# Modulation steps over both halves of each FFN, and a fifth direct block

## The chip, the core and the metric

The kernel runs on one core of a Trainium2 chip. PE is the matrix engine, with its weight loads shown apart; DVE, ACT and POOL are the vector, scalar and general-purpose engines; SP issues most of the DMAs. The time is device microseconds of one execution; a kernel's time is the median of its runs.

## What is computed

Two layers act on 256 latent and 256 context tokens of width 1024 (batch 1), with the same weights for both streams: a half-step SwiGLU feed-forward network (FFN) of 2816 hidden features, a mixer of three head groups, and a second FFN. Each branch has a norm whose shift and scale, and a gate, come from a modulation vector: nine rows of 1024 for each layer and stream, computed from the conditioning vectors.

```python
mod_x = (silu(c) @ ada_w[layer] + ada_b[layer]).reshape(b, 9, 1, d)
mod_c = (silu(c_ctx) @ ada_w[layer] + ada_b[layer]).reshape(1, 9, 1, d)
def ffn_branch(h, mod, i, nw, w1, w2):
    return h + 0.5 * mod[:, i + 2] * swiglu(ada_rms(h, nw, mod[:, i], mod[:, i + 1]), w1, w2)
x   = ffn_branch(x,   mod_x, 0, ...)      # then the mixer with rows 3, 4, 5, then
ctx = ffn_branch(ctx, mod_c, 0, ...)      # ffn_branch(..., 6, ...)
```

The second layer returns latent tokens alone, so its rows 5 to 8 are needed for one stream only.

## The kernel before

**Stages.** There are four FFNs, named here A (layer 0, first), B (layer 0, second), C (layer 1, first) and D (layer 1, second), with a mixer between A and B and between C and D. Tokens of both streams lie side by side, 512 columns; D has the latent 256 columns and two more for the shift.

**One FFN.** Its hidden features are done in two halves of eleven blocks of 128. A half has eleven blocks of the first matrix (a gate product and an up product, each of eight tiles deep) and then eight output tiles of the second matrix, eleven products each. A product is three matmuls, since every weight and activation is split into a high and a low part. The second half ends in a split tail: its last two output tiles are done for latent tokens first and then for context tokens, and the norm of the next stage begins in between.

**Strassen.** In B and C most first-matrix blocks are done by class `Seven`, a scheme with seven half-size products for eight (84 matmuls of 256 columns for 48 of 512). It needs sums of the activations, made once by `sums` on DVE and ACT in the lead of the FFN, and for each block weight sums made by accumulating DMAs of POOL and by DVE. `DIRECT` says how many blocks at the start of B's and C's first half are done directly while the sums are made.

**Weights.** `Stream` (L64) brings chunks in: SP loads a raw chunk (three buffers), ACT casts the high half `wh` (L89), DVE subtracts for the low half `wl` (L100), four buffers each, two chunks for an output tile. Second-matrix weights are prepared one tile ahead. The engines work in the order in which the instructions were written.

**Background steps.** The modulation of the later rows is done by DVE: a block of 128 output rows is a 128 x 1024 tile loaded by DMA, multiplied by the conditioning vector and summed, one instruction (a step, L290) for each stream, followed by a short read of the accumulator; after eight blocks of a row a finish of one or two short instructions. `ada_steps` (L264) lists the loads, steps and finishes; a step issues the load of a block as many blocks ahead as there are buffers. The list `bg` is worked off by `pump` (L185), which each product calls: it adds `pace` for every 512 columns and writes out an entry for each whole one; `drain_bg` writes out all that are left. Layer 0's 112 steps and the first 48 of layer 1 run in A at `APACE`, those of `ADA1` elsewhere: 28 in B's second half and 29 in C's second half with four buffers and loads by POOL, spread up to the tail's last tile, and seven in D's first half with loads by SP.

**Order around the change.** In a second half a tile's products are followed by the result add on DVE (`xT`, L441), the squares for the next norm on ACT (`sq`, L337) and their sum on DVE (`acc`, L341); the next tile's casts and low halves are written after them. In a first half there are no squares. From the sixth tile of B's and C's first half on, SP and POOL also load the weights of the first Strassen block of the second half (`seven.load`, `seven.add`), into the pair of buffers named `aw`.

Of the kernel before, what the change touches and what calls it, by code (L numbers as in the profile page):

```python
# [9 lines left out]
F32 = mybir.dt.float32  # L10
# [10 lines left out]
KT = D // 128  # L21
FF = 2816
JH = FF // 128 // 2
# [12 lines left out]
CHUNK = 1024  # L36
ADA_BUFS = 5

DIRECT = {(0, 1): (4, 0), (1, 0): (4, 0)}

ADA1 = {(0, 0): 48, (0, 1): 27, (1, 0): 29, (1, 1): 8}

STAT, OS, FS, SPR = 3, 3.5, 2, 12

# [6 lines left out]

NM = (4, 2)

SUMS = 1.0
GPACE = (0.4, 0.55)
OPACE = (0.8, 0.8)
APACE = 0.355
NPACE = (0.95, 1.0)
RPACE = (1.2, 1.4)

# [74 lines left out]
def tile_hybrid_dit(ctx: ExitStack, tc: tile.TileContext, t_x, t_c, t_cb, t_ada0, t_ada, t_adab, t_nw, t_w1, t_w2,  # L135
                    t_wi, t_wo, t_qkw, t_bias, t_sgw, t_sgb, t_lnwb, t_lg, t_gnw, t_tab, t_id, t_sel, out):
    nc = tc.nc
    V, S, G, PE, SP = nc.vector, nc.scalar, nc.gpsimd, nc.tensor, nc.sync
# [9 lines left out]
    def mm_bank(name="mm"):  # L148
        return bank("mm", 4, name)
# [8 lines left out]
    for l in range(L):  # L158
        for f in range(2):
            if f == 1:  # L160
                chunks += [t_wi[l, i] for i in WI[l]] + [t_wo[l, m] for m in range(KT)]
            for half in range(2):
                for j in range(DIRECT.get((l, f), (JH, JH))[half]):
                    chunks += [t_w1[l, f, half * JH + j, 0], t_w1[l, f, half * JH + j, 1]]
# [5 lines left out]
    bg = []  # L170
    pace = [0.0, 0.0]
# [26 lines left out]
    def drain_bg(n=None):  # L198
        while bg and (n is None or n > 0):
            bg.pop(0)()  # L200
            if n is not None:
                n -= 1
# [16 lines left out]
    with tc.manual_schedule():  # L219
# [39 lines left out]
        adap = [None, 0, SP, None]  # L259
# [4 lines left out]
        def ada_steps(l, count):  # L264

            def streams(r):

                return 1 if l == L - 1 and r > 4 else 2  # L270

            todo = []
            while ada_todo[l] and sum(streams(r) for r, b in todo) < count:
                todo.append(ada_todo[l].pop(0))
            tiles = {}
            nload = [0]

            def loads(n):
                while nload[0] < min(n, len(todo)):
                    r, b = todo[nload[0]]  # L280
                    t = tiles[r, b] = adap[0](nload[0])
                    adap[2].dma_start(out=t, in_=t_ada[l, r, b])
                    nload[0] += 1

            def step(i, s, n):
                loads(i + adap[1])
                r, b = todo[i]
                t = tiles[r, b]
                junk = adap[3].tile([128, CHUNK], F32, tag="cu", name="junk", bufs=1) if s < n - 1 else t
                V.tensor_tensor_reduce(out=junk, in0=t, in1=cb[:, s], scale=1.0, scalar=0.0, op0=ALU.mult, op1=ALU.add,  # L290
                                       accum_out=mod[l][:, 8 * r + b, s:s + 1])

            def fin(r, n):
                mo = mod[l][:, 8 * r:8 * r + 8, 0:n]
                V.tensor_tensor(out=mo, in0=mo, in1=adab[:, l, 8 * r:8 * r + 8].unsqueeze(2).to_broadcast([128, KT, n]),
                                op=ALU.add)
                i, k = divmod(r, 3)
                if k == 1:
                    V.scalar_tensor_tensor(out=amul[l][:, i, :, 0:n], in0=mo, scalar=1.0,
                                           in1=nw[:, l, i, :].unsqueeze(2).to_broadcast([128, KT, n]),  # L300
                                           op0=ALU.add, op1=ALU.mult)
                elif k == 2 and i != 1:
                    V.tensor_scalar(out=mo, in0=mo, scalar1=0.5, scalar2=None, op0=ALU.mult)

            out = [lambda: loads(adap[1])]
            for i, (r, b) in enumerate(todo):
                n = streams(r)
                out += [lambda i=i, s=s, n=n: step(i, s, n) for s in range(n)]
                if b == KT - 1:
                    out.append(lambda r=r, n=n: fin(r, n))  # L310
            return out
# [313 lines left out]
        def ffn(l, f, lead, norms, steps=None, tail=None):  # L625


            i = 2 * f
            one = lead == "one"
# [3 lines left out]
            with ExitStack() as es:  # L633
                fp = es.enter_context(tc.tile_pool(name="ffn", bufs=1))
                seven = None
                direct = DIRECT.get((l, f), (JH, JH))

# [4 lines left out]
                def seven_pool():  # L642
                    nonlocal seven
                    pool = es.enter_context(tc.tile_pool(name="seven", bufs=1))
                    seven = Seven(pool, fp, l, f)

                if (l, f) in DIRECT:
                    seven_pool()
                else:
                    nb = ADA_BUFS - one  # L650
                    adap[:] = lambda i: fp.tile([128, CHUNK], F32, tag="aw", name="aw", bufs=nb), nb, SP, fp
                if one:
                    bg.extend(ada_steps(1, ADA1[l, f]))
                    pace[0], pace[1] = len(bg) / (KT * (JH - 1)), 0.0
                for half in range(2):
                    aTh = fp.tile([128, JH, NT], F32R, tag="aTh", name="aTh")
# [33 lines left out]
                    if half == 0 and not one:  # L690
# [10 lines left out]
                        if seven:  # L701
                            bg.extend([s for q in range(2) for s in seven.sums(q)])
                            bg.append(lambda: seven.load_u(direct[0]))
                            pace[0], pace[1] = SUMS, 0.0
                        for j in range(2):
# [9 lines left out]
                    for j in range(j0, j1):  # L715
# [4 lines left out]
                        if lead_in and j == j1 - 1:  # L720
                            bg.extend(seven.prepare(n1))
                            pace[0], pace[1] = SUMS, 0.0
                        wg, wu = ws.take(), ws.take(AHEAD - 1)
# [46 lines left out]
                    def down(m, wa, wb, a, b, ps):  # L770
                        for kt in range(JH):
                            w, c = (wa, kt) if kt < 6 else (wb, kt - 6)
                            product(ps[:, a:b], w, 128 * c, aTh, aTl, (slice(None), kt, slice(a, b)),
                                    kt == 0, kt == JH - 1)

                    split_tail = half == 1 and len(streams) == 2
                    if one and half == 0:
                        drain_bg()
                    if seven and half:

                        aw = seven.pool.tile([128, 4, CHUNK], F32, tag="th", name="aw")
                        adap[:] = lambda i: aw[:, i % 4], 4, G, seven.pool
                        bg.extend(ada_steps(1, ADA1[l, f]))
                        pace[0], pace[1] = len(bg) / (JH * (KT - 1)), 0.0
                    ahead = seven and half == 0
                    for m in range(KT - 2 if split_tail else KT):
                        a, b = 0, T * len(streams)
                        wa, wb = ws.take(), ws.take(AHEAD - 1)
                        ps = mm_bank("d")
                        if ahead and m == KT - 3:  # L790
                            seven.load(JH)
                            seven.load(JH + 1)
                            seven.add(JH)
                            seven.add(JH + 1)
                        down(m, wa, wb, a, b, ps)
                        if ahead and m >= KT - 2:
                            for s in seven.prepare(JH)[slice(0, 4) if m == KT - 2 else slice(4, 7)]:
                                s()
                        residual(l, i, m, ps, 0, streams)
                        if half == 1:  # L800
                            for s in streams:
                                if s in norms:
                                    norms[s].add(m)
                            if tail:
                                tail(m)
# [768 lines left out]
        def start(fp, ps, up):  # L1574
# [91 lines left out]
            ws.auto = True  # L1666
            pace[0], pace[1] = APACE, 0.0
            return w
# [30 lines left out]
        for l in range(L):  # L1699
            last = l == L - 1  # L1700
            n1 = {s: Norm(l, 1, s) for s in range(2)}
            n2 = {s: Norm(l, 2, s) for s in range(1 if last else 2)}
            n3 = {} if last else {s: Norm(l + 1, 0, s) for s in range(2)}
            if l == 0:
                bg.extend(ada_steps(0, 112) + ada_steps(1, ADA1[0, 0]))
                bg.insert(1, small_inputs)
                bg.insert(2, lambda: S.activation(out=cb, in_=cb, func=AF.Silu))
                bg.insert(15, prepare)
                pace[0] = 0.0
            ffn(l, 0, "ffn" if l else "start", n1, FFN_TO_MIX)  # L1710
            mixer(l, n2)
            if l == 0:
                ffn(l, 1, "mix", n3, FFN_TO_FFN)
            else:
                def store(m):
                    SP.dma_start(out=out[:, m, :], in_=xT[:, m, 0:T])

                ffn(l, 1, "one", {}, tail=store)
# [117 lines left out]
```

## Time and profile before

| | us |
|---|---|
| runs before | 1841.72, 1845.37, 1847.55 |
| median of the runs | 1845.37 |
| profiled execution | 1841.88 |
| its span | 1840.1 |
| PE, DVE, ACT, POOL busy in the span | 1791.2, 1310.0, 729.4, 262.2 |
| mean granted clock of PE | 0.994 |

The span is the time from the first to the last instruction. All times in rows are microseconds from its start. In a line of instructions the bracket behind a row is the time for which the engine stood idle before it, and what ended that. A granted clock of 1.00 is 2.4 GHz and one of 0.50 is 1.2 GHz. Stretches named in the text: A's second-matrix products of the second half are at 341.8 to 412.1, B's at 1000.6 to 1071.1, C's at 1364.3 to 1439.4; those of B's first half at 828.5 to 890.1 and of C's at 1192.2 to 1253.8; D's first blocks at 1645 to 1710.

### The profile page before, as it was taken

What the parts mean: (1) busy time and instruction counts of PE and PEld (TensorE: products, weight loads), DVE (VectorE), ACT (ScalarE), POOL (GpSimd) and SP (SyncE); (2) the same over time, 40 slices, a digit from 0 to 9 for tenths busy, and PEclk for the clock granted to TensorE, in tenths of its full rate; (3) what the DMA queues carried; (4) which work ended last, traced back from release to release, by engine and by line L of the source; (5) the groups of instructions that cost most, each with busy time, mean ns of one, the idle gap of its engine ahead of it and who ended that gap; (6) DMA issues with size and microseconds to landing.
All of it is one profiled execution on the core that took longest, in us unless ns stands there. A gap on an engine that the chain in (4) does not pass through costs nothing. (4 is left out here: it accounts for less than half of the span.)

```text
span 1840.1 us, 29560 instructions
## 1 busy us (share of the span) xinstructions
PE 1791.2 (97%) x11592; PEld 1556.0 (85%) x11592; DVE 1310.0 (71%) x2214; ACT 729.4 (40%) x1211; POOL 262.2 (14%) x302
## 2 busy tenths in 40 slices
PE   7999999999999999999999999999998999999999
PEld 5787888888668989998999789989996867989999
DVE  5799988886454556783688977836888744667665
ACT  3422222225543234452354245424442555354443
POOL 0000000002014310220322102102212104310000
PEclk9999999999999999999999999999999999999999
DMA  8666766634211121753765626536659432346655
GB/s 310 237 196 221 259 211 215 195 130 149 78 55 47 49 78 58 189 130 124 178 177 175 199 83 169 143 114 184 170 184 317 148 104 76 95 144 234 197 172 157
DMA packets 104763, 292.19 MB, mean 159 GB/s; under 512 B 12208, under 2 KB 18992, under 8 KB 104496
## 3 DMA queue, kind: packets, MB, share of 16 engines
q1 hardware_dynamic: 88352, 249.93, 41.1%
q0 software_dynamic: 16272, 40.38, 10.1%
q8 instruction: 91, 1.49, 0.3%
q14 instruction: 48, 0.39, 0.1%
HBM read 289.21 MB, written 1.05 MB: 158 GB/s over the span
## 5 line engine op out<-in xcount | busy, mean ns | idle before, releaser
L100 DVE TENSOR_TENSOR wl<-wr,wh 128x1024 fp32r<-128x1024 f32 (+2 forms) x304 | 321.9, 1086 | 104.1 <-ACT wh L89 102.7
L89 ACT CAST wh<-wr 128x1024 fp32r<-128x1024 f32 (+2 forms) x304 | 275.8, 932 | 170.4 <-PE d L207 93.7
L206 PE MATMUL d<-aTh,wh 128*128 128x512 f32 (+1 forms) x770 | 273.5, 355 | 12.3 <-ACT wh L89 12.1
L208 PE MATMUL d<-aTh,wl 128*128 128x512 f32 (+1 forms) x770 | 272.8, 354 | 1.9 <-DVE wl L100 1.9
L207 PE MATMUL d<-aTl,wh 128*128 128x512 f32 (+1 forms) x770 | 271.9, 353 | 0.2 <-DVE aTl L682 0.2
L206 PEld LDWEIGHTS d<-aTh,wh 128*128 128x128 f32 x770 | 148.4, 193 | 35.3 <-ACT wh L89 14.1
L208 PEld LDWEIGHTS d<-aTh,wl 128*128 128x128 f32 x770 | 148.0, 192 | 24.9 <-DVE wl L100 4.0
L207 PEld LDWEIGHTS d<-aTl,wh 128*128 128x128 f32 x770 | 148.4, 193 | 21.5 <-DVE aTl L682 0.5
L290 DVE CUSTOM_DVE_ANT_0 aw<-aw,cb 128x1024 f32<-128x1024 f32 x128 | 155.4, 1223 | 7.4 <-DMA aw<-in_ada_dram 4.9
L206 PE MATMUL g<-hTh,wh 128*128 128x512 f32 (+2 forms) x448 | 152.2, 340 | 4.8 <-ACT wh L89 3.8
L208 PE MATMUL g<-hTh,wl 128*128 128x512 f32 (+2 forms) x448 | 151.4, 338 | 3.7 <-DVE wl L100 3.6
L207 PE MATMUL g<-hTl,wh 128*128 128x512 f32 (+2 forms) x448 | 150.9, 337 | 1.3 <-DVE hTl L366 1.1
L208 PE MATMUL u<-hTh,wl 128*128 128x512 f32 (+2 forms) x448 | 150.1, 335 | 0.4 <-DVE wl L100 0.4
L206 PE MATMUL u<-hTh,wh 128*128 128x512 f32 (+2 forms) x448 | 149.8, 334 | 0.0
L207 PE MATMUL u<-hTl,wh 128*128 128x512 f32 (+2 forms) x448 | 149.7, 334 | 0.0
L214 PE MATMUL nat<-wh,hTh 128*128 128x512 f32 (+2 forms) x384 | 137.1, 357 | 0.0
L216 PE MATMUL nat<-wh,hTl 128*128 128x512 f32 (+2 forms) x384 | 127.8, 333 | 0.4 <-DVE hTl L366 0.4
L215 PE MATMUL nat<-wl,hTh 128*128 128x512 f32 (+2 forms) x384 | 127.7, 332 | 0.0
L582 PE MATMUL p<-hTh,wl 128*128 128x256 f32 x432 | 123.8, 287 | 1.0
L582 PE MATMUL p<-th,wl 128*128 128x256 f32 x432 | 121.7, 282 | 0.0
L581 PE MATMUL p<-hTl,wh 128*128 128x256 f32 x432 | 121.4, 281 | 0.0
L580 PE MATMUL p<-hTh,wh 128*128 128x256 f32 x432 | 121.1, 280 | 0.0
(262 smaller groups left out, 4107.9 us busy)
## 6 DMA issues: line engine op xcount, KB each, us to landing
wr<-in_w_dram SPq DMA_DIRECT2D x140, 512.0 KB, 4.4
aw<-in_ada_dram SPq DMA_DIRECT2D x103, 512.0 KB, 4.9
wr<-in_wi_dram SPq DMA_DIRECT2D x56, 512.0 KB, 3.6
wr<-in_w_dram SPq DMA_DIRECT2D x64, 384.0 KB, 3.6
aw<-in_ada_dram POOLq DMA_DIRECT2D x41, 512.0 KB, 5.3
wr<-in_w_dram SPq DMA_DIRECT2D x64, 320.0 KB, 2.9
q<-in_w_dram SPq DMA_DIRECT2D x72, 256.0 KB, 3.6
q<-in_w_dram POOLq DMA_DIRECT2D x72, 256.0 KB, 5.5
```

The costliest lines, as they stand in the source:

```text
L89: self.nc.scalar.copy(out=h[:, :n], in_=self.raw[i][:, :n])
L100: self.nc.vector.tensor_tensor(out=lo[:, :n], in0=t[:, :n], in1=h[:, :n].bitcast(F32), op=ALU.subtract)
L206: PE.matmul(out=ps, lhsT=wh[:, col:col + 128], rhs=hh[rhs_sl], start=start, stop=False)
L207: PE.matmul(out=ps, lhsT=wh[:, col:col + 128], rhs=hl[rhs_sl], start=False, stop=False)
L208: PE.matmul(out=ps, lhsT=wl[:, col:col + 128], rhs=hh[rhs_sl], start=False, stop=stop)
L214: PE.matmul(out=ps, lhsT=hh[lhs_sl], rhs=wh[:, wc], start=start, stop=False)
L215: PE.matmul(out=ps, lhsT=hh[lhs_sl], rhs=wl[:, wc], start=False, stop=False)
L216: PE.matmul(out=ps, lhsT=hl[lhs_sl], rhs=wh[:, wc], start=False, stop=stop)
L290: V.tensor_tensor_reduce(out=junk, in0=t, in1=cb[:, s], scale=1.0, scalar=0.0, op0=ALU.mult, op1=ALU.add, accum_out=mod[l][:, 8 * r + b, s ...
L580: PE.matmul(out=ps, lhsT=wh[:, cw], rhs=th, start=n == 0, stop=False)
L581: PE.matmul(out=ps, lhsT=wh[:, cw], rhs=tl, start=False, stop=False)
L582: PE.matmul(out=ps, lhsT=wl[:, cw], rhs=th, start=False, stop=n == 3)
```

## The change

Layer 1's 112 steps are divided anew: 40 in A, 16 in each half of B and of C during the second-matrix products, eight in D. In a first half the steps use two buffers of the tag `aw` and end, by pace and by a drain, before the sixth tile; in a second half they keep the four buffers and are paced to end with the sixth tile, two tiles before the last. All of them, D's too, are loaded by POOL's queue. In D eight empty entries stand ahead of the steps, so that they fall into the second part of the blocks. B and C have five direct blocks and six Strassen blocks in their first half. The pace of Strassen's sums falls from 1.0 to 0.65 entries a product, that of A's background list from 0.355 to 0.345.

```diff
-DIRECT = {(0, 1): (4, 0), (1, 0): (4, 0)}
-ADA1 = {(0, 0): 48, (0, 1): 27, (1, 0): 29, (1, 1): 8}
+DIRECT = {(0, 1): (5, 0), (1, 0): (5, 0)}
+ADA1 = {(0, 0): (40, 0), (0, 1): (16, 16), (1, 0): (16, 16), (1, 1): (8, 0)}
-SUMS = 1.0
+SUMS = 0.65
-APACE = 0.355
+APACE = 0.345
-                    adap[:] = lambda i: fp.tile([128, CHUNK], F32, tag="aw", name="aw", bufs=nb), nb, SP, fp
+                    adap[:] = lambda i: fp.tile([128, CHUNK], F32, tag="aw", name="aw", bufs=nb), nb, G if one else SP, fp
                 if one:
-                    bg.extend(ada_steps(1, ADA1[l, f]))
+                    bg.extend([lambda: None] * 8 + ada_steps(1, ADA1[l, f][0]))
                     pace[0], pace[1] = len(bg) / (KT * (JH - 1)), 0.0
...
-                    if seven and half:
-                        aw = seven.pool.tile([128, 4, CHUNK], F32, tag="th", name="aw")
-                        adap[:] = lambda i: aw[:, i % 4], 4, G, seven.pool
-                        bg.extend(ada_steps(1, ADA1[l, f]))
-                        pace[0], pace[1] = len(bg) / (JH * (KT - 1)), 0.0
+                    if seven:
+                        if half:
+                            aw = seven.pool.tile([128, 4, CHUNK], F32, tag="th", name="aw")
+                            adap[:] = lambda i: aw[:, i % 4], 4, G, seven.pool
+                        else:
+                            adap[:] = (lambda i: seven.pool.tile([128, CHUNK], F32, tag="aw", name="aw", bufs=2), 2, G,
+                                       seven.pool)
+                        bg.extend(ada_steps(1, ADA1[l, f][half]))
+                        pace[0], pace[1] = len(bg) / (JH * (KT - 2 if half else KT - 3)), 0.0
                     ahead = seven and half == 0
                     for m in range(KT - 2 if split_tail else KT):
...
                         if ahead and m == KT - 3:
+                            drain_bg()
                             seven.load(JH)
...
-                bg.extend(ada_steps(0, 112) + ada_steps(1, ADA1[0, 0]))
+                bg.extend(ada_steps(0, 112) + ada_steps(1, ADA1[0, 0][0]))
```

## Rows read from the trace of the kernel before

**Rows 1.** The page's busy line: us, share of the span, instructions.

```profile
PE 1791.2 (97%) x11592; PEld 1556.0 (85%) x11592; DVE 1310.0 (71%) x2214; ACT 729.4 (40%) x1211; POOL 262.2 (14%) x302
```

**Rows 2.** Waits of PE: who waited for whom, total us, times, longest.

```profile
PE d L206 <- ACT wh L89: 12.1, 3, 6.6
...
PE g L206 <- ACT wh L89: 3.8, 4, 2.1
PE g L208 <- DVE wl L100: 3.6, 8, 0.8
```

**Rows 3.** Windows: length, busy PE, PEld, DVE, ACT, POOL, clock, DMA share, GB/s.

```profile
341.80:412.10 70.30, 66.38 (x342) 56.80 (x341) 59.43 (x106) 19.01 (x34) 0.70 (x1) 0.95 0.46 150
828.50:890.10 61.60, 61.60 (x267) 49.49 (x266) 24.13 (x35) 14.70 (x19) 4.87 (x5) 1.00 0.48 142
1000.60:1071.10 70.50, 66.33 (x342) 56.66 (x341) 60.83 (x108) 19.19 (x35) 8.33 (x15) 0.95 0.58 190
1192.20:1253.80 61.60, 61.60 (x267) 49.48 (x266) 22.88 (x35) 14.50 (x19) 4.90 (x5) 1.00 0.46 140
1364.30:1439.40 75.10, 67.10 (x343) 55.68 (x342) 62.32 (x114) 19.11 (x35) 15.09 (x28) 0.95 0.78 268
```

**Rows 4.** A window at the end of B's second half.

```profile
1053.90:1060.60 6.70, 6.45 (x28) 6.15 (x29) 6.12 (x11) 1.05 (x3) 0.00 (x0) 0.50 0.49 157
```

**Rows 5.** DVE in order of time, B's second half: start, us, what.

```profile
1019.96 1.70 DVE L100 TENSOR_TENSOR wl<-wr,wh 128x768 fp32r<-128x768 f32 x2 [0.30 <-ACT wh L89]
1021.57 1.22 DVE L290 CUSTOM_DVE_ANT_0 aw<-aw,cb 128x1024 f32<-128x1024 f32 x1
...
1026.27 0.87 DVE L441 SCALAR_TENSOR_TENSOR xT<-d,mod,xT 128x256 f32<-128x256 f32 x2
1027.24 0.82 DVE L341 TENSOR_TENSOR acc<-acc,sq 128x256 f32<-128x256 f32 x2
1028.36 1.70 DVE L100 TENSOR_TENSOR wl<-wr,wh 128x768 fp32r<-128x768 f32 x2 [0.30 <-ACT wh L89]
```

**Rows 6.** The same order, the add after B's sixth tile.

```profile
1051.80 0.87 DVE L441 SCALAR_TENSOR_TENSOR xT<-d,mod,xT 128x256 f32<-128x256 f32 x2
```

**Rows 7.** The same order, B's first half.

```profile
844.09 0.88 DVE L441 SCALAR_TENSOR_TENSOR xT<-d,mod,xT 128x256 f32<-128x256 f32 x2 [5.22 <-PE d L208]
```

**Rows 8.** PE in order of time, the first norm's sums.

```profile
8.28 1.01 PE L350 MATMUL ss<-ones,sq 128*128 128x1 f32 x4 [8.28 <-DVE sq L1615]
```

**Rows 9.** PE in order of time, the leads of B and C.

```profile
733.89 0.50 PE L206 MATMUL g<-hTh,wh 128*128 128x512 f32 x1 [2.10 <-ACT wh L89]
...
1097.59 0.50 PE L206 MATMUL g<-hTh,wh 128*128 128x512 f32 x1 [0.69 <-ACT wh L89]
```

**Rows 10.** DVE in order of time, the first sums of B.

```profile
724.40 1.29 DVE L488 TENSOR_TENSOR sum<-hTh,hTl 128x512 f32<-128x512 f32 x2
```

**Rows 11.** Windows: a direct block and a Strassen block.

```profile
745.93:757.07 11.14, 11.14 (x50) 9.02 (x48) 9.43 (x14) 4.91 (x7) 2.77 (x3) 1.00 0.91 233
1151.29:1161.59 10.30, 10.23 (x85) 10.03 (x84) 8.40 (x12) 5.09 (x8) 3.07 (x3) 1.00 0.74 183
```

**Rows 12.** The page's DMA issues; then tile aw from 1000 to 1064.

```profile
aw<-in_ada_dram POOLq DMA_DIRECT2D x41, 512.0 KB, 5.3
...
L282 POOL DMA_DIRECT2D aw<-in_ada_dram x14: 540/540/611, 1001.1 to 1048.6; - x14
...
DMA to landing us min/median/max: 3.9/4.6/6.9
```

**Rows 13.** DVE in order of time, D's first half.

```profile
1684.65 2.36 DVE L100 TENSOR_TENSOR wl<-wr,wh 128x1024 fp32r<-128x1024 f32 x2 [0.53 <-ACT wh L89]
...
1691.04 2.36 DVE L100 TENSOR_TENSOR wl<-wr,wh 128x1024 fp32r<-128x1024 f32 x2 [0.52 <-ACT wh L89]
```

**Rows 14.** Waits of PE from 1645 to 1712.

```profile
PE g L208 <- DVE wl L100: 2.6, 6, 0.8
```

**Rows 15.** The chain that ended last, its longest pieces in order of time.

```profile
1657.38 8.05 DMA wr<-in_w_dram
```

## The prediction

> **What bounds the kernel now.** First the page's busy line: PE works in 97% of the span [rows 1], so time can only be won where PE waits, where its clock is low, or by streaming fewer columns. Next the list of PE's waits [rows 2]: the largest is the second-matrix products waiting for ACT's high half of a weight chunk, 12.1 us in three waits, the longest 6.6; then the first-matrix products waiting for high and low halves. Next the second-matrix stages in one table [rows 3]: the first halves of FFN B and C take 61.6 us each, with DVE busy about 24 of them; the second halves of A, B and C take 70.3, 70.5 and 75.1 for the same products, with DVE busy about 60. Their granted clock is 0.95: behind each of the three waits lies a stretch at 0.50, that is 1.2 GHz; one of the three is in [rows 4].
>
> Why DVE makes PE wait: in one output tile of B's second half [rows 5] DVE does two low halves (1.70), four steps (1021.57 to 1026.27, 1.18 each), result adds and square sums, and the next tile's low halves start 8.40 us after this one's. A tile of products is 61.6/8 = 7.7. So DVE falls back 0.7 us a tile, the result adds come later, ACT's squares wait for them, and the casts of the next weights stand behind the squares on ACT. In B the add of the sixth tile is at 1051.80 [rows 6], though the products should have ended at 1000.6 + 6 x 7.7 = 1046.8: 5 us late. In a first half DVE idles 5.22 us a tile before its add [rows 7].
>
> **Second halves.** Without lateness I expect 61.6 plus the norm's narrow matmuls, which a first half lacks; four of them took 1.01 [rows 8], so 1.0 as an estimate, and 0.5 for small waits: 63.1.
> B: 16 steps and one finish over 66 products make 3 steps a tile, so DVE's round is 8.40 - 1.18 = 7.2 against 7.7: it keeps up, and the last two tiles have no step. Gain 70.5 - 63.1 = 7.4.
> C: 16 steps, two finishes, 3.2 entries a tile, and 16 loads for 25. 75.1 - 63.1 = 12.0; 0.3 kept for waits on loads: 11.7.
> A: the pace falls to 0.345, so 23 entries instead of 24 fall into these six tiles, and one instead of five behind them. Most tiles still have four, more than fit; counted tile by tile (+0.7 with four, -0.5 with three) the last add is 2.8 us late instead of 4.2, so that of the wait 1.2 stays, and 0.7 for the low half behind it. I take no low clock after it, since a wait of 2.10 in B's lead [rows 9] left the clock high. Gain 70.3 - 63.1 - 1.9 = 5.3.
> Together 24.4; bounds 28 if all lateness goes, 16 if A keeps its clock drop and C a wait of 3 us.
>
> **Lead.** Ahead of B's first gate eight entries of Strassen's sums run on DVE, two in 1.29 us [rows 10], 0.64 each; ACT's Silu, the gated product and the cast of the next weights come behind them, and PE waits 2.10 in B and 0.69 in C [rows 9], up to 0.8 more in each for the low half [rows 2]. At pace 0.65 five entries stand ahead of the gate: 3 x 0.64 = 1.9 earlier. Gain 1.9 in B and 1.3 of C's 1.5: 3.2 (bounds 1.5 and 4.4).
>
> **Fifth direct block.** A direct block takes 11.14 us, a late Strassen block of a first half 10.30 [rows 11]; there PE was busy 10.23 with gaps for low halves. 0.84 twice: 1.7 lost. If the removed block would run at PE's own pace, 84 matmuls of half the columns at half of 11.14/48 = 9.75, it is 2.8.
>
> **First halves.** This is what the trace doesn't show: steps there, with two load buffers, issued by POOL. Pace 18/55 (B) and 19/55 (C) gives a step about every 3 products, 2.1 and 2.0 us. DVE's own time fits: 3.6 x 1.18 = 4.3 of the idle 5.22. The loads may not: a buffer is read, reloaded, read again. In B's second half POOL's loads landed a median 4.6 us after issue, 3.9 to 6.9 [rows 12]. With an estimated 0.3 until POOL issues, a two-stream block holds its buffer 4.6 + 0.3 + 2.4 = 7.3; two buffers give four steps in that time, 1.8 a step: it keeps up. All of B's are of this kind: cost 0. In C the last eight steps are of row 5, with one stream: 4.6 + 0.3 + 1.2 = 6.1 for two steps, 3.05 a step against 2.0, and the lateness grows to 8 x 1.05 = 8.4. Behind the waiting step stand, in DVE's order, the result add and the next low halves, and for those PE waits. They may be late by a tile and two matmuls less the add and the first low half: 7.7 + 0.4 - 0.9 - 1.0 = 6.2. So C pays 2.2. The queues passed: POOL's accumulating loads for the next Strassen block stand behind these loads, and SP's loads into the same two buffers wait for the last steps; both come about as much later as PE itself, so 0. Bounds: 0 (landing 3.9) and 17.6 (landing 6.9 throughout: 8 x 2.2, plus 8 x 0.4 in the two-stream steps, less 6.2, plus 3 for a low clock).
> The Trainium skill (DMA: Bandwidth & Descriptors, section Anatomy of one DMA — SWDGE (gpsimd) path) gives 2.0 us plus bytes over 436 GB/s for such a load, an estimate of 3.2 for 512 KB. By it C's first half would cost nothing and the sum would be 2.2 lower; the landings of [rows 12] are longer, and they decide.
>
> **Last FFN.** Eight steps instead of seven, all in the last five blocks, and the loads on POOL. DVE's round with one step took 6.39 [rows 13], so 5.2 without; PE's block is 48 matmuls of 258 columns, 5.6 by the direct block's pace. 8 x 1.18 - 5 x 0.4 = 7.4 late, of which about 2 are cover (the low halves are done that long before they are needed): 5.4. Before, PE waited 2.6 for low halves [rows 14] and about as much again in restarts and casts, 4.5; part of it came from a weight load of 8.05 that shared SP with four modulation loads [rows 15], which goes, since POOL is free to issue long before. 1.0 lost (bounds 2 gained, 3 lost).
>
> **Sum.** -24.4 - 3.2 + 1.7 + 2.2 + 1.0 = -22.7 against the profiled execution's own 1841.9 (span 1840.1): 1819.2. That execution is 3.5 under the median of the runs, 1845.4; the median to expect is 1822.7.
>
> **Rivals.** (1) Landings in the first halves are slower, some 6.9: C pays 15.4 more; 1838. For it: the page's median over all POOL loads is 5.3 [rows 12]; against it: the first halves move 140 GB/s, the second halves 190 and 268 [rows 3].
> (2) Slower than before: in the same two-buffer loop the landing sets the pace of both first halves. At x us a single-stream step costs (x + 1.5)/2, a two-stream one (x + 2.7)/4; less 6.2 of cover in each half and plus the low clock, that eats the whole gain from x = 7.7 on; at 9 it costs about 37 and the time is 1857. No such median in the trace.
> (3) The second halves' waits are not the steps' but the chain of add, square, cast and low half itself, some 3.3 us against the half tile of 3.85: then they stay, and with the other terms the time is 1847. Against it: the growing lateness [rows 5, 6].
> (4) The lead's waits stay, because the gate is held up by something else: 1826.
> (5) POOL's issues are held up while DVE works, by one step in each loop, 3.65 a step in C: 4.8 more; 1828. The trace has every issue at 0.54 to 0.61 us in a stretch in which DVE was busy [rows 12], which speaks against this.
> The Trainium skill (SBUF — State Buffer, section SBUF: two separate sides) warns of (5): loads issued by GpSimd can starve while a DVE operation holds the ports that both share.
>
> **Chances and range.** Forecast 0.74 (its own range 1814 to 1832), (1) 0.08, (2) 0.04, (3) 0.05, (4) 0.06, (5) 0.03. A change of 0.3%, 5.5 us, is about what a measurement of this kernel can tell from none. Faster by more: 0.74 + 0.06 + 0.03 + 0.06 of (1) = 0.89; within: 0.05 + 0.02 of (1) = 0.07; slower 0.04. The range takes in the bounds of the second halves and of the last FFN and most of (1): 1812 to 1836.
>
> **What would show it.** Right: in the windows the second halves of B and C near 63 us at a clock of 1.00, A's near 65; PE's wait for ACT ahead of second-matrix products down from 12.1 to about 3; in C's first half DVE waits for modulation loads and a PE stall of some 2 us at the seventh tile. Wrong: low-clock stretches at the ends of B and C as before; first halves well over 64 us; DVE waiting for loads in B's first half; the waits of the leads unchanged.

## The result and the profile after

The changed kernel takes 1815.05 us (median of 4 runs, 1813.16 to 1815.47), the kernel before 1843.55 (4 runs, 1839.45 to 1847.55): a ratio of 0.9844, 95% interval 0.9819 to 0.9868, 28.5 us faster. The forecast was 1822.7, 22.7 under the median then known, 1845.4. The profiled execution of the changed kernel has a span of 1813.7 against 1840.1, 26.4 less; the rest of the 28.5 is that the profiled execution of before lay 1.7 under its median and that of the changed kernel 0.4 above.

The page's busy line and the list of PE's waits answer [rows 1, 2]:

```profile
PE 1782.3 (98%) x11520; PEld 1547.3 (85%) x11520; DVE 1300.8 (72%) x2200; ACT 725.3 (40%) x1203; POOL 260.7 (14%) x307
```

POOL's loads of modulation rows rise from 41 to 52. They are those of B, C and D; the loads of the 40 steps in A stay on SP.

```profile
PE yt L1507 <- POOL yR L1298: 2.5, 1, 2.5
...
PE g L208 <- DVE wl L100: 1.9, 3, 0.8
PE d L208 <- DVE wl L100: 1.9, 4, 0.9
...
PE g L206 <- ACT wh L89: 1.1, 3, 0.5
PE d L206 <- ACT wh L89: 1.1, 1, 1.1
```

The second-matrix products' wait for ACT's high half is down from 12.1 to 1.1, a single wait, in A; the first-matrix products' waits fell from 3.8 to 1.1 and from 3.6 to 1.9. The windows of the same stages answer [rows 3] (length, busy PE, PEld, DVE, ACT, POOL, clock, DMA share, GB/s); in their order: A's second half, B's first and second half, C's first half, the Strassen blocks behind it, C's second half, D's first half with its products.

```profile
341.50:406.30 64.80, 63.24 (x341) 53.74 (x340) 54.66 (x98) 19.02 (x34) 0.70 (x1) 1.00 0.48 152
819.40:881.00 61.60, 61.60 (x266) 49.51 (x265) 42.10 (x69) 14.94 (x19) 8.05 (x11) 1.00 0.64 184
991.40:1054.10 62.70, 62.70 (x342) 53.61 (x341) 47.34 (x84) 19.22 (x35) 5.08 (x9) 1.00 0.50 163
1173.10:1235.80 62.70, 61.84 (x266) 49.44 (x265) 39.14 (x65) 13.05 (x18) 10.01 (x15) 1.00 0.68 211
1235.80:1348.30 112.50, 111.72 (x925) 109.88 (x925) 91.98 (x122) 55.62 (x88) 28.58 (x28) 1.00 0.63 161
1348.30:1411.00 62.70, 62.70 (x342) 53.62 (x342) 47.38 (x86) 19.22 (x35) 9.24 (x17) 1.00 0.67 230
1612.30:1714.90 102.60, 98.17 (x801) 96.11 (x800) 71.92 (x114) 46.86 (x66) 5.03 (x9) 1.00 0.66 207
```

In the second halves of B and C PE is now busy for the whole window, 62.70 of 62.70, at a clock of 1.00, with DVE at 47 us instead of 61 and 62. In B's first half DVE rose from 24 to 42 us and nothing was lost.

From here a stage runs from its first matmul to the first matmul of the next stage, in PE's order of time; "lead to end" of B and C is the lead, the direct and the Strassen blocks of the first half together. In us:

| stage | before | after | difference | forecast |
|---|---|---|---|---|
| A, second half | 70.29 | 64.84 | -5.45 | -5.3 |
| B, second half | 70.47 | 62.72 | -7.75 | -7.4 |
| C, second half | 75.10 | 62.72 | -12.38 | -11.7 |
| B, lead to end | 122.06 | 118.87 | -3.19 | -1.06 |
| C, lead to end | 121.08 | 118.98 | -2.10 | -0.46 |
| B, first-half products | 61.60 | 61.60 | 0 | 0 |
| C, first-half products | 61.60 | 62.72 | +1.12 | +2.2 |
| C, Strassen behind them | 110.47 | 112.50 | +2.03 | 0 |
| D, all | 201.02 | 201.41 | +0.39 | +1.0 |
| mixer of layer 1 | 199.71 | 201.23 | +1.52 | 0 |
| A, first-half products | 62.21 | 61.60 | -0.61 | 0 |
| all else | | | 0.0 | 0 |

The table adds up to -26.4. The lead terms are the forecast's gains of 1.9 and 1.3 with its +0.84 for a block each. In the mixer a granted clock of 0.50 shows from 1589.95 on, in work that the change leaves alone:

```profile
1589.90:1593.40 3.50, 3.45 (x16) 3.45 (x17) 0.69 (x2) 1.41 (x2) 0.00 (x0) 0.51 0.03 5
```

### The profile page after: what moved, and what is told of

It is laid out like the page before. It is cut to its first block, busy times and chain, and to the rows that moved or that the text cites. A ratio compares the mean times of both kernels' runs of the same rounds, so it can differ in the third digit from the quotient of the medians.

```text
span 1813.7 us, 29366 instructions
## 1 busy us (share of the span) xinstructions
PE 1782.3 (98%) x11520; PEld 1547.3 (85%) x11520; DVE 1300.8 (72%) x2200; ACT 725.3 (40%) x1203; POOL 260.7 (14%) x307
## 5 line engine op out<-in xcount | busy, mean ns | idle before, releaser
L290 DVE CUSTOM_DVE_ANT_0 aw<-aw,cb 128x1024 f32<-128x1024 f32 x128 | 155.6, 1223 | 11.7 <-DMA aw<-in_ada_dram 9.1
L206 PE MATMUL g<-hTh,wh 128*128 128x512 f32 (+2 forms) x464 | 158.4, 341 | 2.1 <-ACT wh L89 1.1
L208 PE MATMUL g<-hTh,wl 128*128 128x512 f32 (+2 forms) x464 | 157.4, 339 | 2.0 <-DVE wl L100 1.9
L207 PE MATMUL g<-hTl,wh 128*128 128x512 f32 (+2 forms) x464 | 157.3, 339 | 1.3 <-DVE hTl L366 1.1
L208 PE MATMUL u<-hTh,wl 128*128 128x512 f32 (+2 forms) x464 | 156.6, 337 | 0.4 <-DVE wl L100 0.4
L206 PE MATMUL u<-hTh,wh 128*128 128x512 f32 (+2 forms) x464 | 156.1, 336 | 0.0
L207 PE MATMUL u<-hTl,wh 128*128 128x512 f32 (+2 forms) x464 | 156.1, 336 | 0.0
L290 DVE CUSTOM_DVE_ANT_0 junk<-aw,cb 128x1024 f32<-128x1024 f32 x96 | 117.0, 1219 | 4.4 <-DMA aw<-in_ada_dram 4.0
L582 PE MATMUL p<-hTh,wl 128*128 128x256 f32 x408 | 116.2, 285 | 0.7
L582 PE MATMUL p<-th,wl 128*128 128x256 f32 x408 | 114.7, 281 | 0.3 <-DVE wl L551 0.3
L581 PE MATMUL p<-hTl,wh 128*128 128x256 f32 x408 | 114.6, 281 | 0.0
```

What stands on the lines that cost most here:

```text
L206: PE.matmul(out=ps, lhsT=wh[:, col:col + 128], rhs=hh[rhs_sl], start=start, stop=False)
L207: PE.matmul(out=ps, lhsT=wh[:, col:col + 128], rhs=hl[rhs_sl], start=False, stop=False)
L208: PE.matmul(out=ps, lhsT=wl[:, col:col + 128], rhs=hh[rhs_sl], start=False, stop=stop)
L581: PE.matmul(out=ps, lhsT=wh[:, cw], rhs=tl, start=False, stop=False)
L582: PE.matmul(out=ps, lhsT=wl[:, cw], rhs=th, start=False, stop=n == 3)
```

## The experiments

Totals of single executions scatter: the four runs of the kernel before lie 8.1 us apart, eight of the changed kernel 4.6 (1812.67 to 1817.29). In the traces much of it lies in stretches at half clock (a granted clock of 0.50) in the mixers and in A, and in A's first blocks, which lie outside the edits. So the stages decide, and the totals stand beside them. Each variant below was run once, the last one five times.

### Lead: the two edits one by one

**The fifth direct block alone**, on the kernel before:

```diff
-DIRECT = {(0, 1): (4, 0), (1, 0): (4, 0)}
+DIRECT = {(0, 1): (5, 0), (1, 0): (5, 0)}
```

> The kernel before with the fifth direct block alone. Theory (head start): the chain of DVE and ACT work behind one Strassen block takes 10.3 us whatever else runs and PE needs 9.93, so PE waits only once DVE's head start is used up; a direct block of 11.14 leaves DVE idle and gives it a head start of about 2 us more, so that the six blocks of the first halves run at 9.93. Lead plus Strassen of B's first half then 122.1 + 0.84 - 4 x 0.37 = 121.4, of C's 121.1 + 0.84 - 1.5 = 120.4; the lead's waits (2.10 and 0.69) stay; the kernel 1.3 us under the one before. Rival (the prediction's term): blocks stay at 10.3, B 122.9, C 121.9, the kernel 1.7 us over it.

1845.04, beside 1844.53 for the kernel before. Lead to end: B 122.94 (+0.88), C 121.28 (+0.20). About the whole time of the extra block came back from the Strassen blocks: seven took 71.43, the remaining six 59.55 in B, 9.93 each, and 60.39 in C, where the last two took 10.3. In the kernel before, the blocks of both first halves took 9.92, 10.01, and from then on 10.3 [rows 11]. The lead's wait of 2.10 stayed, and this time the clock went low behind it:

```profile
736.35 0.50 PE L206 MATMUL g<-hTh,wh 128*128 128x512 f32 x1 [2.11 <-ACT wh L89]
```

```profile
738.30:741.70 3.40, 3.40 (x10) 2.62 (x9) 2.70 (x5) 1.12 (x2) 0.00 (x0) 0.50 0.83 260
```

These 3.4 us at half clock make B's lead about 1.6 longer than the extra block does. They can't simply be taken off, since DVE gets ahead while PE is slow: in e3_steps below, with four direct blocks, the same stretch lies in B's lead, the Strassen blocks take 70.54 instead of 71.43, and lead to end is 122.10 against 122.06 without it. So C, which kept its clock, gives the price of the block alone: 0.2. The forecast had +0.84 in each.

**The slower sums alone**, on the kernel before:

```diff
-SUMS = 1.0
+SUMS = 0.65
```

> The kernel before with the pace of Strassen's sums at 0.65 alone, four direct blocks. Theory (head start): the lead's waits go (about 2.3 us in B, 1.3 in C), but the sums and the first block's preparation no longer fit into the four direct blocks, some five entries are written out at their end, and the Strassen blocks start without head start: all seven at 10.3 and a wait at their beginning; lead plus Strassen about 121 to 122 in B and 121 in C. Rival (the terms are independent, as the prediction summed them): 122.1 - 2.3 = 119.8 in B and 121.1 - 1.3 = 119.8 in C.

1848.31, beside 1844.53. Lead to end: B 123.64 (+1.58), C 121.91 (+0.83): slower, which neither theory had. The wait ahead of the gate went, as forecast, but four direct blocks are too few for the sums at this pace. The preparation of the first Strassen block stands behind the sums in the same background list; now it is reached only by the drain, so its low halves are written behind the last direct block's gated product, and there PE waits. PE first, then DVE, in order of time:

```profile
755.49 0.28 PE L581 MATMUL p<-hTl,wh 128*128 128x256 f32 x1
758.89 0.58 PE L582 MATMUL p<-hTh,wl 128*128 128x256 f32 x1 [3.12 <-DVE wl L551]
```

```profile
754.12 0.69 DVE L494 SCALAR_TENSOR_TENSOR tl<-sum,th 128x512 fp32r<-128x512 f32 x1 [0.70 <-ACT th L491]
755.64 0.69 DVE L675 TENSOR_TENSOR sg<-sg,u 128x512 f32<-128x512 f32 x1 [0.82 <-PE u L208]
757.01 0.69 DVE L682 TENSOR_TENSOR aTl<-sg,aTh 128x512 fp32r<-128x512 f32 x1 [0.68 <-ACT aTh L679]
757.62 1.22 DVE L551 TENSOR_TENSOR wl<-wr,wh 128x1024 fp32r<-128x1024 f32 x1
```

In the kernel before, that low half started at 754.76, 2.3 us ahead of the first Strassen matmul at 757.07; here at 757.62, 2.3 us behind it at 755.37. From within this wait on B's clock stood at 0.50 for 6.8 us, which is in its 1.58; C kept its clock, so its 0.83 is the clean figure.

```profile
757.80:764.60 6.80, 5.71 (x26) 5.71 (x27) 4.09 (x4) 2.86 (x5) 2.42 (x2) 0.50 0.24 80
```

The two edits together gain 3.19 and 2.10, each alone loses; in C, without low clock, 0.20 and 0.83. They are one measure: the slower pace needs the fifth block to finish the list in, and the fifth block gains nothing alone while the gate waits.

**The new division of the steps alone**, the changed kernel with both lead edits undone:

```diff
-DIRECT = {(0, 1): (5, 0), (1, 0): (5, 0)}
+DIRECT = {(0, 1): (4, 0), (1, 0): (4, 0)}
-SUMS = 0.65
+SUMS = 1.0
```

> The changed kernel with four direct blocks and the sums' pace of before: the new division of the steps alone. Theory (steps per tile set DVE's round, and that sets PE's waits): second halves 64.8, 62.7 and 62.7 us with no low clock at their ends, as in the changed kernel; C's first half 62 to 64; B's and C's lead plus Strassen 122.1 and 121.1 as before; about 1819 to 1820 us. Rival (the waits of the second halves are the chain of add, square, cast and low half, and went with the other parts of the change): second halves near 70 again, 1840 us or more.

1829.98, 10 over what was expected. By stages, the second halves of B and C are 62.72 each, as in the changed kernel, and lead to end 122.10 and 121.08, as in the kernel before: 5.3 of the 14.5 above the changed kernel. The rest lies in stages that the edit leaves alone: 3.2 in the mixer of layer 0 (294.2 to 294.4 in the other executions), with the clock at 0.50 from 619.4 to 626.2, 1.5 in A behind a short wait, 1.6 in the mixer of layer 1, 2.7 up to the end of A's first half, 0.7 in C's first half.

**A sixth direct block** in the changed kernel:

```diff
-DIRECT = {(0, 1): (5, 0), (1, 0): (5, 0)}
+DIRECT = {(0, 1): (6, 0), (1, 0): (6, 0)}
```

> The changed kernel with a sixth direct block in B and C. Theory (a Strassen block takes 9.93 as long as DVE has a lead over PE and 10.30 when it has none; after the fifth direct block all six run at 9.93): the sixth direct block gains nothing and costs 11.14 - 9.93 = 1.2 in each FFN, lead and Strassen blocks of B's first half 120.1 (118.9 with five), C's 120.2 (119.0), total 2.4 higher. Rival (direct blocks go on paying): 118.9 or less in each.

Lead to end 120.07 in B (+1.20) and 119.80 in C (+0.82); the total, 1815.75, hides it. Of the two only B's is clear of scatter: with five direct blocks lead to end took 118.82 to 118.87 there, but 118.70 to 119.45 in C. It is the plain price of the exchange in B: a direct block of 11.13 for a Strassen block that ran at PE's own 9.93. The fifth block was worth it because the blocks that it relieved ran at 10.3, and the sixth has nothing to relieve. The windows show a Strassen block in each condition, first the last of B's first half, then a late one of C's second half, both of the changed kernel:

```profile
809.49:819.42 9.93, 9.93 (x86) 9.93 (x85) 8.69 (x14) 4.98 (x9) 1.94 (x3) 1.00 0.65 219
1317.43:1327.76 10.33, 10.24 (x87) 10.04 (x85) 8.42 (x12) 5.10 (x8) 3.04 (x3) 1.00 0.69 178
```

DVE is not full in either, 8.4 of 10.33. In order of time, the preparation of a block (DVE's work with its waits for ACT's casts and POOL's sums) repeats every 10.3, in quick blocks and slow ones alike; PE needs 9.93. The time by which DVE is done with a block before PE needs it is called its head start here. PE eats 0.37 of it in each block and pays 0.37 a block when it is gone. The repeating 10.3 is read from the order; no run changed it by itself.

### Second halves: number of steps or early end

**As many steps as after, ending one tile later**, as before:

```diff
-pace[0], pace[1] = len(bg) / (JH * (KT - 2 if half else KT - 3)), 0.0
+pace[0], pace[1] = len(bg) / (JH * (KT - 1 if half else KT - 3)), 0.0
```

> The changed kernel, with the steps of the second halves of B and C spread over all tiles but the last one (as before) instead of ending two tiles ahead; their number stays 16 each. Theory (the number of steps in a tile decides, not where they end): 17 or 18 entries over 77 products are 2.2 to 2.4 a tile, DVE's round stays under the 7.7 us of a tile, so both second halves stay at 62.7 (up to 63.2), no low clock at their ends, total 1815 within 2. Rival (the early end is what takes the wait away, since add, square, cast and low half of the last tile are a chain of their own): 64 to 66 in each, total 1818 to 1822.

1812.95; both second halves at 62.72, not 0.01 off:

```profile
990.70:1053.40 62.70, 62.70 (x342) 53.62 (x341) 47.46 (x84) 19.16 (x35) 5.07 (x9) 1.00 0.49 163
1346.40:1409.10 62.70, 62.70 (x342) 53.62 (x341) 47.23 (x85) 19.18 (x35) 9.24 (x17) 1.00 0.68 230
```

**As many steps as before, ending two tiles ahead**, as after:

```diff
-ADA1 = {(0, 0): (40, 0), (0, 1): (16, 16), (1, 0): (16, 16), (1, 1): (8, 0)}
+ADA1 = {(0, 0): (40, 0), (0, 1): (5, 27), (1, 0): (3, 29), (1, 1): (8, 0)}
```

> The changed kernel with the old number of steps in the second halves (27 in B, 29 in C; 5 and 3 in their first halves), still ending two tiles ahead. Theory (the number of steps in a tile decides): 28 entries over six tiles are 4.7 a tile, DVE's round 8.4 + 0.7 x 1.18 = 9.2 against 7.7, so 9 us late after six tiles, of which some 2 are covered: B's second half about 69 to 71 and C's 72 to 76, with PE waiting for ACT's high halves around the sixth tile and a stretch at low clock behind it; total 1832 to 1836, less 2 in C's first half and its following Strassen blocks, which have hardly any loads then: these go back to 61.6 and 110.5. Rival (the early end decides): both second halves 63 to 65, total 1814 to 1818.

1845.75. The steps come out as 6 and 28 in B, 4 and 29 in C, and 5 in D; the second halves have as many as in the kernel before. B's takes 74.88 and C's 82.79, both longer than before. Crowded into six tiles, the steps make DVE's round, from one tile's low halves to the next one's, 9.67 where five of them stand in it:

```profile
1014.39 1.70 DVE L100 TENSOR_TENSOR wl<-wr,wh 128x768 fp32r<-128x768 f32 x2 [0.30 <-ACT wh L89]
...
1021.98 0.87 DVE L441 SCALAR_TENSOR_TENSOR xT<-d,mod,xT 128x256 f32<-128x256 f32 x2
...
1024.06 1.69 DVE L100 TENSOR_TENSOR wl<-wr,wh 128x768 fp32r<-128x768 f32 x2 [0.30 <-ACT wh L89]
```

and the wait for the high half is back, with the clock at 0.95 and 0.92 over the two stages:

```profile
1053.46 0.58 PE L206 MATMUL d<-aTh,wh 128*128 128x256 f32 x1 [6.11 <-ACT wh L89]
```

```profile
993.40:1068.20 74.80, 66.06 (x342) 54.87 (x341) 61.49 (x110) 19.15 (x35) 8.29 (x15) 0.95 0.55 179
1359.30:1442.10 82.80, 71.34 (x342) 58.80 (x341) 62.82 (x114) 19.15 (x35) 15.57 (x29) 0.92 0.74 250
```

So the number of steps decides. Ending two tiles ahead gives nothing where the steps are few and harms where they are many.

Fewer steps are also fewer loads. In B the loads are not the cause: neither DVE nor ACT waits for a DMA in its second half, in the kernel before or here. In C a part of the lateness is theirs. DVE's waits up to the stall, first of the kernel before, then here:

```profile
DVE aw L290 <- DMA aw<-in_ada_dram: 3.9, 2, 2.0
```

```profile
DVE aw L290 <- DMA aw<-in_ada_dram: 6.7, 5, 2.2
```

**A's steps faster**, to be done sooner in its second half:

```diff
-APACE = 0.345
+APACE = 0.38
```

> The changed kernel with A's pace at 0.38 instead of 0.345: A's steps end within the first two tiles of its second half. Theory (A's remaining wait of 1.24 and 0.65 for the high and the low half comes from four steps a tile): it goes, A's second half falls from 64.8 to 62.7 to 63.2, A's first half stays at 61.6 or rises by up to 0.5, total 1.9 lower. Rival (the wait is the tail's own chain): 64.8 again.

1826.01, a miss of both theories. The wait at the sixth tile did go, but the pace holds for A's first-matrix blocks too. There DVE now falls behind, and each of A's second-matrix stages begins with a wait for the last block's activations; the second is followed by a stretch at half clock:

```profile
169.09 0.50 PE L206 MATMUL d<-aTh,wh 128*128 128x512 f32 x1 [1.59 <-ACT aTh L679]
...
357.20 0.49 PE L206 MATMUL d<-aTh,wh 128*128 128x512 f32 x1 [3.15 <-ACT aTh L679]
```

A's first-half products take 64.29 instead of 61.60, the second half 68.25 instead of 64.84. The same kind of lateness, smaller, cost the kernel before 0.6 in A's first half at 0.355; that is the -0.61 in the table.

### C's first half: one-stream blocks

**The rows of layer 1 in another order**, so that C's first half gets blocks used by two streams only:

```diff
-ada_todo = [[(r, b) for r in range(2 if l == 0 else 0, 9) for b in range(KT)] for l in range(L)]
+full = lambda *rs: [(r, b) for r in rs for b in range(KT)]
+r4 = full(4)
+ORDER = [full(*range(2, 9)), full(0, 1, 2) + full(3)[:4] + full(5, 6) + full(3)[4:] + r4 + full(7, 8)]
+ada_todo = [[(r, b) for r, b in ORDER[l]] for l in range(L)]
```

> The changed kernel with the rows of layer 1 in another order, so that both first halves have blocks with two steps each and the single-step blocks lie in the second halves with four buffers; as many steps everywhere as in the changed kernel. Theory (in C's first half two buffers can't reload single-step blocks in time): C's first half falls from 62.7 to 61.6, and the Strassen blocks behind it from 112.5 to about 110.5, since DVE no longer starts them late; 3 us in all. Rival (it is DVE's time for the steps, or the loads' traffic): 62.7 and 112.5 stay.

The total, 1815.63, shows nothing. The stages show all of it: C's first half 61.60 (-1.12) and the Strassen blocks behind it 110.70 (-1.80). What swallowed 4.2 lies in A: 2.5 in its first blocks, and 1.7 behind its remaining wait, where the clock went low:

```profile
395.14 0.38 PE L206 MATMUL d<-aTh,wh 128*128 128x256 f32 x1 [1.26 <-ACT wh L89]
```

```profile
397.00:400.40 3.40, 3.40 (x18) 3.40 (x18) 1.78 (x4) 0.42 (x1) 0.00 (x0) 0.50 0.88 295
```

DVE's waits in C's first half, first of the changed kernel, then with the new order:

```profile
DVE aw L290 <- DMA aw<-in_ada_dram: 9.1, 5, 3.2
```

```profile
DVE junk L293 <- DMA aw<-in_ada_dram: 0.2, 1, 0.2
```

### D: empty entries and queue

**Without the eight empty entries**, so that the eight steps spread over the whole half:

```diff
-bg.extend([lambda: None] * 8 + ada_steps(1, ADA1[l, f][0]))
+bg.extend(ada_steps(1, ADA1[l, f][0]))
```

> The changed kernel without the eight empty entries in D: its eight steps are spread over all blocks of the first half, as before, with the loads still issued by GpSimd. Theory (the empty entries crowd two steps into the last blocks, which costs 1.3 in the following product stage, 32.1 against 30.8): D's first half and first product stage together 101.3 instead of 102.6, total 1.3 lower. Rival (DVE falls behind by the sum of the steps wherever they stand, and the queue makes no difference): 102.5, as in both kernels.

D's first half and its products take 100.92. With D as in the changed kernel they took 102.58 there and 102.30 to 102.48 in six other executions, so the entries cost 1.4 to 1.7 here. In e8_all below, also without them, the two take 101.39, which makes it 0.9 to 1.2. The total, 1817.57, again has a half-clock stretch in A and slow first blocks.

**D's loads back on SP:**

```diff
-adap[:] = lambda i: ..., nb, G if one else SP, fp
+adap[:] = lambda i: ..., nb, SP, fp
```

> The changed kernel with D's modulation loads issued by SyncE again, between the weight loads. Theory of the prediction (weight loads are held up by modulation loads in the same queue): D's first half and first product stage together 103 to 104 instead of 102.6, with a weight load of about 8 us in the chain. Rival (the queue makes no difference, the steps' own time on DVE does): 102.6, or up to 0.5 less.

104.28 instead of 102.3 to 102.6, so POOL's queue is worth 1.7 to 2.0 in this one execution. On SP the first four loads go at 1643.82, between weight loads; on POOL they go from 1618.5 on. The first step waits for its load. A weight load in the chain takes 7.06 (about 8 was expected), its cast comes late, and the two low halves of the next weights are torn apart by it:

```profile
1648.07 7.06 DMA wr<-in_w_dram
```

```profile
1650.12 1.23 DVE L290 CUSTOM_DVE_ANT_0 aw<-aw,cb 128x1024 f32<-128x1024 f32 x1 [0.94 <-DMA aw<-in_ada_dram]
1654.25 1.23 DVE L100 TENSOR_TENSOR wl<-wr,wh 128x1024 fp32r<-128x1024 f32 x1 [0.53 <-ACT wh L89]
1656.31 1.23 DVE L100 TENSOR_TENSOR wl<-wr,wh 128x1024 fp32r<-128x1024 f32 x1 [0.84 <-ACT wh L89]
```

### A version put together

The new row order, no empty entries in D, and four steps moved from A to B's first half, timed beside the changed kernel:

```diff
-ADA1 = {(0, 0): (40, 0), (0, 1): (16, 16), (1, 0): (16, 16), (1, 1): (8, 0)}
+ADA1 = {(0, 0): (36, 0), (0, 1): (20, 16), (1, 0): (16, 16), (1, 1): (8, 0)}
```

> The changed kernel itself, as the reference of this group: 1812 to 1816, 28 under the kernel before.

> A version put together from the findings: (a) the modulation rows of layer 1 reordered so that C's first half gets only two-stream blocks; (b) no empty entries in D; (c) four steps moved from A (36 instead of 40) to B's first half (20 instead of 16), A's pace kept at 0.345, so that A's steps end a tile earlier. By the stages measured with each alone: (a) -2.9 (C's first half 61.6, the Strassen blocks behind it 110.7), (b) -1.3 to -1.6 in D, (c) up to -1.9 in A's second half (64.8 to 63); B's first half stays at 61.6, since 20 two-stream steps at 1.8 us fit into five tiles of 7.7. Together 5 to 6 under the changed kernel, about 1808.5. Rival: the waits are taken up elsewhere, by a low-clock stretch or by loads in B's first half, and the two are equal.

The changed kernel: 1815.34 (4 runs), ratio to the kernel before 0.984, interval 0.9826 to 0.9853. The version: 1811.63 (5 runs, 1809.14 to 1814.75), ratio 0.9819, interval 0.9806 to 0.9832. Its interval lies wholly under 1, so it beats the kernel before; the 3.7 us to the changed kernel are likely, but the two intervals overlap. Stage by stage, against the changed kernel's first profile: A's second half 62.72 (-2.11), C's first half 61.60 (-1.12), its Strassen blocks 110.43 (-2.07), D's first half and products -1.19. Against that, twenty steps are too many for B's first half: 64.51 (+2.91), and its Strassen blocks 112.19 (+1.77).

```profile
849.39 0.50 PE L208 MATMUL d<-aTh,wl 128*128 128x512 f32 x1 [0.85 <-DVE wl L100]
866.60 0.50 PE L208 MATMUL d<-aTh,wl 128*128 128x512 f32 x1 [1.55 <-DVE wl L100]
```

There DVE waits 7.2 us for loads. The expectation's own figure left no room: twenty steps and two other entries over 55 products fall due every 1.75 us, and two buffers were taken to give a step every 1.8. Sixteen steps in B's first half, and the four in A left out of its second half in some other way, is what remains to be tried.

## Why the prediction was right

**Second halves: right, in sum and in cause.** -25.6 against -24.4. Fewer steps a tile let DVE keep up [rows 5, 6], and in C there were fewer loads to wait for, 16 where the kernel before had 27 (the forecast counted 25). In the changed kernel's B a round with three steps is 7.71, the tile's own time, and DVE waits again for PE ahead of the add:

```profile
1024.58 1.70 DVE L100 TENSOR_TENSOR wl<-wr,wh 128x768 fp32r<-128x768 f32 x2 [0.30 <-ACT wh L89]
...
1030.14 0.88 DVE L441 SCALAR_TENSOR_TENSOR xT<-d,mod,xT 128x256 f32<-128x256 f32 x2 [0.30 <-PE d L208]
1031.16 0.82 DVE L341 TENSOR_TENSOR acc<-acc,sq 128x256 f32<-128x256 f32 x2 [0.15 <-ACT sq L337]
1032.29 1.69 DVE L100 TENSOR_TENSOR wl<-wr,wh 128x768 fp32r<-128x768 f32 x2 [0.30 <-ACT wh L89]
```

Rival (3), that the chain of add, square and cast keeps the waits, fell with e4_tail and e9_count, which separate count from place. What the forecast said of the last two tiles without a step was no part of the gain. The base of 63.1 was 0.4 too high. In A the two waits left are 1.24 and 0.65, measured from one matmul's start to the next one's, forecast 1.2 and 0.7.

**A's clock: right in this profile, on a weak ground.** That a wait of 2.10 had left the clock high [rows 9] does not carry over: in e1_direct the same wait was followed by low clock, and so was A's shorter one in six of nine executions. So the -5.45 in A is partly luck: over the nine its second half took 65.9 on the average, 4.4 less than before.

**Lead and fifth block: wrong in sum, -1.5 against -5.3.** Two steps failed. The fifth block's +0.84 compared two blocks [rows 11] and left out that it also gives DVE a head start over the six blocks behind it. Alone it cost 0.20 in C, and 0.88 in B with 3.4 us at half clock; in B the sixth cost 1.20. And the gain of the slower sums was costed as if they could be put off for nothing. The waits ahead of the gate, 2.10 and 0.69, did go with the slower sums alone, so rival (4) fell. But the sums come due at the first Strassen block, and alone they lose 0.83 in C and 1.58 in B, there with 6.8 us at half clock; the fifth block is their room. Terms added one by one can't give this: in C, where no clock fell, the singles sum to +1.0 and the pair is -2.1; with B they sum to +3.5 against -5.3.

**C's first half: the cause right, the price short.** The eight one-stream steps made DVE wait 9.1 for loads (forecast 8.4 late), PE stalled at the seventh tile as said, for 1.02 (forecast 2.2; the stage alone took 62.10 to 63.45 in eight executions, 0.5 to 1.9 more than without steps); in B DVE waited for no load. The landings in C's first half:

```profile
DMA to landing us min/median/max: 3.8/4.1/5.2
```

They are shorter than the 4.6 taken, so rivals (1) and (2) didn't come to pass. By the Trainium skill (DMA: Bandwidth & Descriptors, section Anatomy of one DMA — SWDGE (gpsimd) path) the estimate was 3.2; no such load landed in under 3.65 in any run. What the step missed is what lies behind: the "cover" of 6.2 that it let DVE use up for nothing is the head start of the Strassen blocks. In the kernel before seven of the eleven blocks ran at 9.93 and the eighth was the first slower one; in the changed kernel the first took 10.45 and the fifth was slow again. That eighth block, then that fifth one:

```profile
1323.34:1333.45 10.11, 10.11 (x86) 10.05 (x86) 8.20 (x12) 5.10 (x8) 3.07 (x3) 1.00 0.66 173
1276.09:1286.28 10.19, 10.19 (x87) 10.03 (x85) 8.29 (x12) 5.09 (x8) 3.04 (x3) 1.00 0.70 172
```

They lost 2.03 in all. In e5_rows most of it, 1.80, came back when the loads' wait went, and in e9_count, with four steps there, 1.77. Both together vary from execution to execution: in eight with this order of rows C's first half and the Strassen blocks behind it took 173.6 to 175.9, 1.5 to 3.9 more than in the kernel before. "Both come about as much later as PE itself, so 0" was the wrong sentence.

**D: right, for the reasons given.** +0.39 against +1.0. D as a whole scatters by about as much as this (200.05 to 201.02 in three executions of before's, 200.59 to 201.41 in seven of the changed kernel's), so the parts show more than the sum: the crowding costs 0.9 to 1.7 (e6_d_spread, e8_all), the queue gives 1.7 to 2.0 (e11_d_sp), and the two nearly cancel. Rival (5) found no support: POOL's loads of modulation rows were issued in 0.53 to 0.62 us each in every run, with DVE at work. The starving that the Trainium skill (SBUF — State Buffer, section SBUF: two separate sides) warns of shows in no run here.

**Not forecast:** the 1.52 in the mixer of layer 1. It is chance and not the change: with the same mixer instructions the stage took between 199.7 and 202.9 in these runs, with one or two stretches at half clock or none.

**The sum.** The forecast was 7.6 above the median, and the median lies near the fast end of the range that the forecast had for itself, 1814 to 1832. In the stages 3.7 more was gained than forecast: 3.8 in the lead, 1.2 in the second halves, 0.6 each in D and in A's first half, less 1.0 in C and 1.5 in the mixer. The rest is the allowance of 3.5 for a profile under its median; the changed kernel's profile, 1815.47, was not.

## What to carry to other kernels

Count the background work of the engine that feeds the bottleneck tile by tile, and move what doesn't fit to stages where that engine idles; where in the stage it ends matters little. Slack that such an engine builds up is not free to spend: ask which later stage lives on it, and take edits that spend it and edits that give it back as one term. And compare stages, not totals, when the effect is of the size of the clock's scatter.

## What the runs showed of the hardware

The same short wait does not always cost the same. At A's sixth tile nine executions with the same steps show one wait of PE of 0.8 to 1.3 us. Behind it the granted clock stayed at 1.00 in three of them, and A's second half took 64.6 to 65.0; in six it fell to 0.50 for 3.4 us, and the half took 66.3 to 66.6. A's first eleven blocks differ as well, between 136.4 and 139.7 where their instructions are the same. It goes with the moment from which PE is fast. At first a matmul of 512 columns takes 0.63 us, as in a recorded stretch at 0.50 (e1_direct, 24.91 to 31.74), and later 0.39 or 0.40. Where the blocks took 136.4, PE is fast by 25.8 at the latest; where they took 139.0 or more, from 31.3 to 32.6 on. First e8_all (136.41), then e5_rows (139.70):

```profile
21.34 0.63 PE L207 MATMUL g<-hTl,wh 128*128 128x512 f32 x1
25.79 0.39 PE L208 MATMUL g<-hTh,wl 128*128 128x512 f32 x1
```

```profile
29.08 0.63 PE L208 MATMUL u<-hTh,wl 128*128 128x512 f32 x1
32.19 0.39 PE L208 MATMUL g<-hTh,wl 128*128 128x512 f32 x1
```

What makes the clock rise earlier or later is not shown.
